# A decoder layer on one core: seven of eleven gate-and-up groups computed as Strassen block products, and the recurrence's stores issued one step later

## The chip, the cores and the metric

The kernel runs on one core of a Trainium2 chip. Five engines work side by side and meet at semaphores: TensorE (PE in the tables; its weight loads are listed apart as PEld), VectorE (DVE), ScalarE (ACT), GpSimd (POOL) and SyncE (SP), which here only issues transfers (DMAs). The metric is the time of one execution on the device in microseconds (us), lower is better.

## The reference, cut to what matters

```python
    lru = _rglru_branch(lru_x, lru_gate, conv_w, conv_b, lru_wa, lru_ba, lru_wi, lru_bi, lru_lambda)
    merged = merge_g[:, :, 0] * (attn @ w_o_attn) + merge_g[:, :, 1] * (lru @ w_o_lru)
    x = x + merged @ w_out
    h2 = _rmsnorm(x, norm2_g)
    return x + (jax.nn.silu(h2 @ w_gate) * (h2 @ w_up)) @ w_down
```

There are 512 tokens and 1024 channels; `w_gate` and `w_up` are 1024 x 2816, `w_down` is 2816 x 1024. All is float32. The recurrence (`_rglru_branch`) is a convolution, two sigmoid gates out of small matrix products, coefficients, a scan over the tokens and a product with a gelu gate.

## The kernel before, in words

**Products.** A float32 operand is cut in two: `hi`, its rounding to the matmul's type (a copy on ACT), and `lo`, the rest (a subtraction on DVE). One product is then three matmuls, hi by hi, lo by hi, hi by lo (`mm3`, lines 197 to 199). Each of them loads its own 128 x 128 weights.

**Weights.** They lie packed in the order of use, in chunks of 128 x 1024 (512 KB). `Weights.load` issues a chunk's transfer on SP into a `raw` tile; `cut_steps` makes `whi` (L165, ACT) and `wlo` (L168, DVE) of it; `get` hands the parts out and cuts and loads some chunks ahead. Five pairs of parts are in flight. Every engine executes its instructions in the order in which the code issues them, so a wait of one instruction holds up all behind it on that engine; SP's transfers too are issued in that order.

**Recurrence.** For each of eight blocks of 128 channels: a projection into a PSUM bank, `lru_conv`, `lru_parts` (hi and lo of the convolved block, L187 and L188), `lru_gates` (six matmuls into two `ps_s` banks), `lru_coeffs` (four ACT functions beginning at L370, then DVE work that ends in `tv` and `av`), `lru_scan`, then `lru_out` and `lru_store` (two transfers of 256 KB into the DRAM tensor `lru_d`). The last blocks overlap with the next stages: four projections `acck` for the compression's keys and values, `blocks_add` and `blocks_split` (tiles `shifted`, `blkh`, `blkl`), then a loop of six steps, each with a projection for the merge gates, `merge_gate` of the step before (ACT L497 reads its bank, SP stores the result in `mg_d`), and one or two chunks of the compression's first layer `w1` (256 columns, into `ps_s`). After it comes the token-major projection of the keys; its four accumulators need all four `ps_dense` banks, the fourth only after `merge_gate(5)` has read it.

**Second norm.** `out_mm` adds the output projection up in eight PSUM banks, two to each of four token blocks. `norm2_sums(t)` adds `x` to them (DVE L1146) and squares and sums (ACT L1147), POOL multiplies by the gain; `norm2_scale(t)` scales; `norm2_t(t)` transposes block t by eight matmuls into two banks and splits them into `h2h` and `h2l`, the norm's result with channels on partitions. `x2`, the sum, stays in SBUF until the end.

**Gate and up.** 22 tiles of 128 output channels, two units each (gate, up); a unit is 8 x 3 matmuls of 512 columns (all tokens). The first three units are split in two halves of 256 tokens, so that they can start while blocks 2 and 3 are still being transposed. After each pair: silu on ACT (L1218), product on DVE (L1219), hi and lo of the result (`gh`, `gl`).

**Down.** Two passes over 22 tiles, each into four token blocks by 512 channels; then `x2` is added and the result stored.

Of the kernel before, what the change touches and what calls it, by code (L numbers as in the profile page):

```python
# [18 lines left out]
P = 128  # L19
# [80 lines left out]
def hybrid_block_kernel(ctx: ExitStack, tc: tile.TileContext, x: bass.AP, wpk: bass.AP,  # L100
# [25 lines left out]
    class Weights:  # L126
# [11 lines left out]
        def load(self, upto):  # L138
            while self.loaded <= min(upto, len(keys) - 1):
# [9 lines left out]
        def cut_steps(self, upto, on_hi=None, on_lo=None, n_steps=1):  # L149
            while self.cut_ <= min(upto, self.stop - 1):  # L150
# [427 lines left out]
    for c in range(N_EARLY):  # L578
        prev, acc = acc, proj_cm(cm("w_in", C_MERGE + P * c), ahead=2)
        if c:  # L580
            merge_gate(c - 1, None, prev)
# [24 lines left out]
        outs = ((), (), (0, 1), (2, 3, 4), (5, 6), (7,))[c]  # L606
# [505 lines left out]
    def late_pool(**kw):  # L1112
        p_, es = open_pool(**kw)
        ctx.enter_context(es)
        return p_

    stage3 = late_pool(name="stage3", bufs=3, side="right")
    x2p = late_pool(name="x2p", bufs=1)
    h2p = late_pool(name="h2p", bufs=1)
    gp = late_pool(name="gp", bufs=28)  # L1120
    fp = late_pool(name="fp", bufs=2, side="right")
    ps = late_pool(name="ps_ffn", bufs=8, space=PSUM)
    PS.clear()
    PS.update(b=8)
    W.stage((stage2, stage3, stage3, stage2, stage3), (stage2, stage3, stage2, stage3), (dve,))
    x2 = x2p.tile([P, NT, D], F32, name="x2")
    for t in range(NT):
        nc.sync.dma_start(x2[:, t, :], x[t * P:(t + 1) * P, :])

    def wkey(name, h, c):  # L1130
        return cols(name, ((512 * h, 512 * h + 512),), 2 * c, 2)

    h2q = [[h2p.tile([P, 4, T], F32R, name=f"h2{m}{b}") for m in "hl"] for b in range(2)]
    h2T = [[m[:, k % 4, :] for m in h2q[k // 4]] for k in range(KT)]
    xn2, sums = {}, {}

    halves = (slice(0, 512), slice(512, D))
    gain2 = [gp.tile([P, 512], F32, tag="g", name="gain2") for _ in halves]
    for sl, g in zip(halves, gain2):
        nc.sync.dma_start(g, rows[:, 640 + sl.start:640 + sl.stop])  # L1140

    def norm2_sums(t):
        xn2[t] = [gp.tile([P, 512], F32, tag="g", name="xn2") for _ in halves]
        ss, v0, w0 = [fp.tile([P, 2], F32, tag="n" + m, name="n" + m, bufs=2) for m in "svw"]
        for h, sl in enumerate(halves):
            dve.tensor_tensor(out=x2[:, t, sl], in0=x2[:, t, sl], in1=acc[t][h], op=OP.add)  # L1146
            act.activation(fp.tile([P, T], F32, tag="sg", name="sq"), x2[:, t, sl], AF.Square,  # L1147
                           accum_out=ss[:, h:h + 1])
            pool.tensor_tensor(out=xn2[t][h], in0=x2[:, t, sl], in1=gain2[h], op=OP.mult)
# [24 lines left out]

    late = 3
# [5 lines left out]
    W.cut(W.used + 1)  # L1181
    for t in range(NT):
# [8 lines left out]
        norm2_sums(t)  # L1191
        if t == 2:
            norm2_t(0)
    norm2_scale(3)


    gT = []
    units = [(n, i) for i in range(FT) for n in ("w_gate", "w_up")]
    early = 3
    w, acc = [], []  # L1200
    for n, i in units[:early]:
        w.append(W.get(cm(n, P * i), KT, ahead=0))
        acc.append(bank("b"))
        mm_cm(acc[-1], w[-1], h2T, lo_half, between=(lambda: norm2_t(len(w))) if len(w) > 1 else None)
    gate_acc = None
    for n, (name, i) in enumerate(units):
        if n < early:
            a = acc[n]
            mm_cm(a, w[n], h2T, hi_half)
            W.cut(W.used)  # L1210
        else:
# [97 lines left out]
```

## Time and profile before

| what | value |
|---|---|
| median of 3 runs | 994.64 us (994.56 to 995.04) |
| the profiled execution | 996.74 us, of which the span of instructions 995.0 us |
| PE busy, and PEld | 976.8 us (98% of the span), 817.1 us |
| DVE busy | 558.2 us (56%) |
| ACT busy | 473.0 us (48%) |
| mean granted TensorE clock | 0.998 of full speed |

The profiled execution is 2.1 us longer than the median and its span 0.4 us longer. A busy share is the time in which an engine had an instruction in work; PE's is modelled from pipelined instructions, so the distance from one start to the next (the pitch) says more than a duration. The stages, by the starts of their first matmuls: recurrence and projections up to about 240 us, attention up to about 575, output projection and second norm up to 620, gate and up 620.1 to 868.5, down 868.5 to 992.

### The profile page before, as it was taken

How to read it: one execution, taken by the hardware profiler on the slowest of the kernel's cores; microseconds unless marked ns; L12 is line 12 of the kernel's file. 1: busy time of each engine (PE TensorE's matmuls, PEld its weight loads, DVE VectorE, ACT ScalarE, POOL GpSimd, SP SyncE). 2: the span in 40 equal slices, each digit the busy share in tenths (PEclk: the TensorE clock that was granted, in tenths of full speed). 3: DMA queues.
4: the chain of work that ended last, by engine and by line, in shares of the span. 5: the costliest groups of instructions: out<-in, count | busy, mean ns of one | idle time of the engine just before them, and what ended most of it. 6: DMA issues, size and time to landing. Idle time of an engine off the chain costs nothing.

```text
span 995.0 us, 13201 instructions
## 1 busy us (share of the span) xinstructions
PE 976.8 (98%) x4915; PEld 817.1 (82%) x4915; DVE 558.2 (56%) x1056; ACT 473.0 (48%) x887; POOL 179.5 (18%) x252
## 2 busy tenths in 40 slices
PE   6999999899999999999999999999999999999998
PEld 6888778788898888888888888988888888888887
DVE  6775998638666787878875545533333333331311
ACT  7556767445655777767763334432223222222110
POOL 2031110113302455545541003100000000000000
PEclk9999999999999999999999999999999999999999
DMA  6321427642223121621214481223222332241501
GB/s 235 99 81 61 135 82 236 228 138 71 73 77 116 44 65 54 223 62 35 64 55 125 139 315 45 85 85 111 101 85 85 93 119 85 85 137 55 172 19 42
DMA packets 34479, 104.84 MB, mean 105 GB/s; under 512 B 3952, under 2 KB 4336, under 8 KB 34416
## 3 DMA queue, kind: packets, MB, share of 16 engines
q1 hardware_dynamic: 34416, 104.01, 32.2%
q8 instruction: 38, 0.62, 0.3%
q14 instruction: 25, 0.20, 0.1%
HBM read 93.51 MB, written 10.49 MB: 105 GB/s over the span
## 4 chain that ended last, share of the span: by engine, by line
PE 79%; DVE 6%; ACT 3%; issue 2%; DMA 1%; ACTq 0%; DVEq 0%
PE ps_b L199 14%; PE ps_b L198 14%; PE ps_b L197 14%; PE ps_dense L1020 10%; PE ps_t L911 4%; PE ps_s L198 2%; PE ps_s L199 2%; PE ps_s L197 2%; PE ps_dense L197 2%; PE ps_dense L199 2%; PE ps_dense L198 2%; PE ps_s L880 2%; PE ps_s L881 2%; PE ps_pv L939 2%; PE ps_pv L938 2%
## 5 line engine op out<-in xcount | busy, mean ns | idle before, releaser
L168 DVE TENSOR_TENSOR wlo<-raw,whi 128x1024 fp32r<-128x1024 f32 (+2 forms) x198 | 185.5, 953 | 109.6 <-ACT whi L165 108.8
L165 ACT CAST whi<-raw 128x1024 fp32r<-128x1024 f32 (+2 forms) x207 | 165.7, 818 | 103.9 <-PE ps_b L199 70.0
L197 PE MATMUL ps_b<-h2h,whi 128*128 128x512 f32 (+1 forms) x376 | 143.4, 381 | 0.0
L199 PE MATMUL ps_b<-h2h,wlo 128*128 128x512 f32 (+1 forms) x376 | 143.2, 381 | 0.0
L198 PE MATMUL ps_b<-h2l,whi 128*128 128x512 f32 (+1 forms) x376 | 143.2, 381 | 0.0
L902 POOL TENSOR_SCALAR p<-p,st,gates 128x128 f32<-128x128 f32 (+3 forms) x128 | 78.5, 626 | 81.0 <-DVE st L898 44.3
L1219 DVE TENSOR_TENSOR sg<-sg,ps_b 128x512 f32<-128x512 f32 x22 | 15.1, 686 | 138.3 <-PE ps_b L199 138.3
L199 PE MATMUL ps_dense<-hth,wlo 128*128 128x512 f32 (+1 forms) x232 | 86.6, 373 | 0.5 <-DVE wlo L168 0.5
L197 PE MATMUL ps_dense<-hth,whi 128*128 128x512 f32 (+1 forms) x232 | 87.0, 375 | 0.0
L198 PE MATMUL ps_dense<-htl,whi 128*128 128x512 f32 (+1 forms) x232 | 86.4, 372 | 0.0
L892 ACT ACTIVATE p<-p,st 128x128 f32<-128x128 f32 (+3 forms) x128 | 72.0, 563 | 24.0 <-DVE st L887 23.4
L199 PEld LDWEIGHTS ps_b<-h2h,wlo 128*128 128x128 f32 x376 | 70.7, 188 | 15.0
L198 PEld LDWEIGHTS ps_b<-h2l,whi 128*128 128x128 f32 x376 | 70.7, 188 | 14.9
L197 PEld LDWEIGHTS ps_b<-h2h,whi 128*128 128x128 f32 x376 | 70.7, 188 | 14.8
L198 PE MATMUL ps_b<-wlo,gh 128*128 128x512 f32 (+1 forms) x198 | 73.2, 370 | 0.0
L199 PE MATMUL ps_b<-whi,gl 128*128 128x512 f32 (+1 forms) x198 | 73.1, 369 | 0.0
L197 PE MATMUL ps_b<-whi,gh 128*128 128x512 f32 (+1 forms) x198 | 73.1, 369 | 0.0
L187 ACT CAST gh<-sg 128x512 fp32r<-128x512 f32 x22 | 13.6, 620 | 123.1 <-DVE sg L1219 123.1
L923 DVE TENSOR_TENSOR ptl<-ps_t,pth 128x512 fp32r<-128x512 f32 x80 | 55.1, 689 | 22.7 <-ACT pth L917 21.7
L887 DVE CUSTOM_DVE_ANT_0 p<-ps_s,bias 128x128 f32<-128x128 f32 (+3 forms) x128 | 61.3, 483 | 10.4 <-PE ps_s L881 7.1
L917 ACT CAST pth<-ps_t 128x512 fp32r<-128x512 f32 x80 | 46.6, 582 | 32.3 <-PE ps_t L911 31.6
L199 PEld LDWEIGHTS ps_dense<-hth,wlo 128*128 128x128 f32 x232 | 43.8, 189 | 9.3 <-DVE wlo L168 0.9
(266 smaller groups left out, 2042.2 us busy)
## 6 DMA issues: line engine op xcount, KB each, us to landing
raw<-in_wpk_dram SPq DMA_DIRECT2D x150, 512.0 KB, 3.6
lru_d<-lt SPq DMA_DIRECT2D x16, 256.0 KB, 4.5
mt<-mg_d SPq DMA_DIRECT2D x16, 256.0 KB, 3.8
mg_d<-mt SPq DMA_DIRECT2D x10, 256.0 KB, 2.1
xt<-in_x_dram SPq DMA_DIRECT2D x4, 512.0 KB, 5.7
lh<-lru_d SPq DMA_DIRECT2D x8, 256.0 KB, 4.1
ll<-lru_d SPq DMA_DIRECT2D x8, 256.0 KB, 4.3
x<-in_x_dram SPq DMA_DIRECT2D x4, 512.0 KB, 6.2
```

Of the source, the lines that this page charges most:

```text
L165: (on_hi or act.copy)(hi[:, sl], raw[:, sl])
L168: eng.tensor_tensor(out=lo[:, sl], in0=raw[:, sl], in1=f(hi[:, sl]), op=OP.subtract)
L197: pe.matmul(acc, lhsT=ah, rhs=bh, start=start, stop=False)
L198: pe.matmul(acc, lhsT=ah, rhs=bl, start=False, stop=False)
L199: pe.matmul(acc, lhsT=al, rhs=bh, start=False, stop=stop)
L887: dve.tensor_tensor_reduce(out=p, in0=accs.pop((h, br, t)), in1=bias[h][:, 384 - t * P:512], scale=-1.0, scalar=3e38, op0=OP.add, op1=OP.m ...
L892: act.activation(p, p, AF.Exp, bias=stat[h][:, 0, br, t:t + 1], scale=-1.0, accum_out=stat[h][:, 1, br, t:t + 1])
L902: pool.tensor_scalar(p, p, sm[:, t:t + 1], gates[:, t, c:c + 1], op0=OP.mult, op1=OP.mult)
L911: pe.transpose(pt[:, o_:o_ + P], probs[h, br, t][:, k * P:(k + 1) * P], ident)
L917: act.copy(ph, pts[h, gi][0])
L923: dve.tensor_tensor(out=pl, in0=pt, in1=f(ph), op=OP.subtract)
L1020: pe.matmul(acc, lhsT=a[l], rhs=b[r], start=start and i == 0, stop=stop and i == 2)
```

## The change

**Gate and up.** Two output tiles (128 channels each, gate and up side by side) make a group; eleven groups. Group 0 is computed plainly, in halves of 256 tokens, as four units (`unit`). Groups 3, 6 and 9 are computed plainly with 512 columns. The other seven are a 2 x 2 block product, weights A (rows: the two tiles, columns: the two halves of the 1024 inputs) by h2 B (rows: halves of the inputs, columns: halves of the tokens), by seven products in place of eight. A product is 24 matmuls for gate and up together (two halves of a bank) by 256 columns. The sums of weights (S1 to S4, 128 x 1024) are made by DVE for each group (`adds`) ahead of their hi and lo; the sums of B (T1 to T4) once, at the end of the second norm (`norm2_t`, `late_sums`, `sum_parts`); the products are added to the four corners by seven additions of 128 x 512 out of PSUM (`post`), and silu and product follow on corners of 256 columns (`gated`). The weights' `raw` tiles now come as pairs (two chunks, three pairs in flight). A step s of the loop issues product s, the sum for s+4, the hi and lo for s+3, and the corner work of s-1. The hi and lo of the results are made later, in the first pass of down (`down_parts`).

**Room.** To make room, `x2` is stored to DRAM (`x2_d`, two buffers in SBUF) and read back near the end of each pass of down; two raw buffers serve the other chunks from the second norm on, where four did; the squares' dump goes into the PSUM bank that was just read.

**Recurrence.** The outputs of two blocks are made at a time (`lru_outs`, lo in place) and their stores issued in the next step (`lru_stores`); the last two come after `merge_gate(5)` and the gelu. `lru_gates(7)` stands one projection later.

```diff
-        for j in outs:
-            lru_out(j)
-        for j in outs:
-            lru_store(j)
+        if 2 <= c < 5:
+            lru_outs(2 * c - 4, 2 * c - 3)
...
+            lru_outs(6, 7)
+            lru_stores()
...
     acck.append(proj_cm(cm("w_in", 1024 + P), ahead=2))
-    lru_gates(7)
     kv_evac(0, acck[0], act.copy)
     lru_scan(4)
     acck.append(proj_cm(cm("w_in", 1024 + 2 * P), ahead=2))
+    lru_gates(7)
...
         prev, acc = acc, proj_cm(cm("w_in", C_MERGE + P * c), ahead=2)
+        lru_stores()
...
-            act.activation(fp.tile([P, T], F32, tag="sg", name="sq"), x2[:, t, sl], AF.Square,
-                           accum_out=ss[:, h:h + 1])
+            act.activation(acc[t][h], v, AF.Square, accum_out=ss[:, h:h + 1])
...
+            bs[t] = [half("b") for _ in range(2)]
+            for d, a in zip(bs[t], pt):
+                act.copy(d, a)
...
+        dve.tensor_tensor(out=t1, in0=pt[0], in1=bs[t - 2][0], op=OP.subtract)
+        dve.tensor_tensor(out=t2, in0=t1, in1=pt[1], op=OP.subtract)
...
+    A_OF = {1: "A11", 2: "A12", 3: "S4", 4: "A22", 5: "S1", 6: "S2", 7: "S3"}
+    B_OF = {1: "B11", 2: "B21", 3: "B22", 4: "T4", 5: "T1", 6: "T2", 7: "T3"}
+    SUMS = {"S1": ("A21", OP.add, "A22"), "S2": ("A11", OP.subtract, "S1"),
+            "S3": ("A21", OP.subtract, "A11"), "S4": ("A12", OP.add, "S2")}
+    NO = FT // 2
+    PLAIN = (0, 3, 6, 9)
+    seq = [(o, p) for o in range(1, NO) for p in ((-1, -2, -3, -4) if o in PLAIN else (1, 5, 2, 6, 7, 3, 4))]
...
+        bh, bl = h2[B_OF[p]]
+        for n in range(2):
+            for k in range(4):
+                sl = slice(512 * n + k * P, 512 * n + k * P + P)
+                mm3(b[:, 256 * n:256 * n + 256], (hi[:, sl], lo[:, sl]), (bh[:, k, :], bl[:, k, :]), k == 0, k == 3)
...
+        elif p == 2:
+            corner(0, 0, 2, 1)
+        elif p == 6:
+            held[2], held[4] = half("u2"), half("u4")
+            add(two(held[2]), 6, 1)
+            add(two(held[4]), 5, 2)
+        elif p == 7:
+            held[3] = half("u3")
+            add(two(held[3]), 7, 2)
+            corner(1, 1, 5, 3)
...
+    def step(s):
+        banks[seq[s][1]] = product(s)
+        adds(s + AHEAD + 1)
+        prep(s + AHEAD)
+        do_later()
+        if s:
+            post(s - 1)
...
+        if t in (1, 2):
+            x2_store(t - 1)
+            x2_load(t + 1)
...
+    AHEAD = 3
+    w, uacc = [], []
+    for n in range(4):
+        i, m = divmod(n, 2)
+        w.append(W.get(cm(("w_gate", "w_up")[m], P * i), KT, ahead=int(n > 0)))
+        uacc.append(bank("b"))
+        unit(uacc[n], w[n], lo_half, {1: lambda: norm2_t(2), 2: lambda: norm2_t(3)}.get(n))
```

Three places show how instructions stand now. The first is on PE in the recurrence's end: the gates of block 7 are the six rows with `ps_s<-lt`, the rows around them are projections into `ps_dense` (`hth`, `htl` are the first norm's parts). Before, they stand between the second and the third of the `acck` projections:

```order
L199 MATMUL ps_dense<-hth,wlo 128x512
L197 MATMUL ps_s<-lt,whi 128x512 [waits Activation_49]
L198 MATMUL ps_s<-lt,whi 128x512 [waits DVE_49]
L199 MATMUL ps_s<-lt,wlo 128x512
L197 MATMUL ps_s<-lt,whi 128x512
L198 MATMUL ps_s<-lt,whi 128x512
L199 MATMUL ps_s<-lt,wlo 128x512
L197 MATMUL ps_dense<-hth,whi 128x512
```

and of the change the same six rows, 24 matmuls (one projection) further on:

```order
L200 MATMUL ps_dense<-hth,wlo 128x512
L198 MATMUL ps_s<-lt,whi 128x512 [waits Activation_49]
L199 MATMUL ps_s<-lt,whi 128x512 [waits DVE_49]
L200 MATMUL ps_s<-lt,wlo 128x512
L198 MATMUL ps_s<-lt,whi 128x512
L199 MATMUL ps_s<-lt,whi 128x512
L200 MATMUL ps_s<-lt,wlo 128x512
L198 MATMUL ps_dense<-hth,whi 128x512 [waits Activation_49]
```

So one projection has moved ahead of them, while on ACT and DVE the coefficients of block 7, which read these banks, keep their place between their neighbours.

The second is on DVE inside gate and up. Before, two units are two `wlo` and one product with its lo:

```order
L168 TENSOR_TENSOR wlo<-raw,whi 128x1024 x2
L1219 TENSOR_TENSOR sg<-sg,ps_b 128x512
L188 TENSOR_TENSOR gl<-sg,gh 128x512
```

Of the change, three steps of a Strassen group that another one follows (`S` is a sum of weights, `c` and `u` corner sums out of PSUM, `g` the silu product; the rows with `wlo` are the lo of a weight or of a sum):

```order
L1254 TENSOR_TENSOR S<-raw_7345,S 128x1024
L189 TENSOR_TENSOR wlo<-raw_7345,whi 128x1024
L1301 TENSOR_TENSOR g<-sg,c 128x256
L1317 TENSOR_TENSOR c<-ps_b,u_7618 128x512
L1254 TENSOR_TENSOR S<-raw_7509,raw_7345 128x1024
L189 TENSOR_TENSOR wlo<-S,whi 128x1024
L1301 TENSOR_TENSOR g<-sg,c 128x256
L1317 TENSOR_TENSOR c<-ps_b,u_7650 128x512
L1254 TENSOR_TENSOR S<-raw_7345,S 128x1024
L189 TENSOR_TENSOR wlo<-S,whi 128x1024
```

Where a unit of 24 matmuls had about two DVE instructions, a product of 24 shorter ones now has about three, 22 to a group.

The third is SP at the second norm. Before, SP has only weights to issue from here on; of the change, the stores and loads of `x` stand between the last two chunks of group 0, and the store of a block ahead of the load that takes its buffer:

```order
L1166 DMA x_d<-x_6148 128x1024 [waits DMAHW2_49,DVE_49]
L1151 DMA x_6404<-in_x_dram 128x1024 [waits DMAHW2_49,DMAHW3_49,Activation_49,Pool_49]
L1166 DMA x_d<-x_6150 128x1024 [waits DMAHW4_49,DVE_49]
L1151 DMA x_6448<-in_x_dram 128x1024 [waits DMAHW4_49,DMAHW5_49,Activation_49,Pool_49]
L145 DMA raw<-in_wpk_dram 128x1024 [waits DMAHW6_49]
L1166 DMA x_d<-x_6404 128x1024 [waits DMAHW7_49,DMAHW3_49,DVE_49]
L1166 DMA x_d<-x_6448 128x1024 [waits DMAHW5_49,DMAHW0_49,DVE_49]
L145 DMA raw<-in_wpk_dram 128x1024 [waits DMAHW1_49]
```

Thus the load of group 0's last chunk stands behind the store that waits for the sum of the last token block.

## Rows read from the trace of the kernel before

**Rows 1.** The page, part 1: busy time of each engine, share, instructions.
```profile
PE 976.8 (98%) x4915; PEld 817.1 (82%) x4915; DVE 558.2 (56%) x1056; ACT 473.0 (48%) x887; POOL 179.5 (18%) x252
```

**Rows 2.** Waits of PE: waiting tile, releaser, us in total, times, longest.
```profile
PE ps_dense L197 <- ACT lt L497: 2.5, 1, 2.5
PE ps_s L198 <- DVE lt L188: 2.0, 2, 1.5
PE ps_dense L199 <- DVE wlo L168: 0.5, 1, 0.5
...
PE ps_s L198 <- DVE wlo L168: 0.3, 1, 0.3
```

**Rows 3.** Timeline of PE: start, duration; first 512-column unit, first of down.
```profile
638.91 0.39 PE L197 MATMUL ps_b<-h2h,whi 128*128 128x512 f32 x1
...
868.51 0.39 PE L197 MATMUL ps_b<-whi,gh 128*128 128x512 f32 x1
```

**Rows 4.** The same, a long stretch of 256-column matmuls, two of its starts.
```profile
629.09 0.28 PE L198 MATMUL ps_b<-h2l,whi 128*128 128x256 f32 x1
...
638.79 0.28 PE L199 MATMUL ps_b<-h2h,wlo 128*128 128x256 f32 x1
```

**Rows 5.** Window: length, busy PE, PEld, DVE, ACT, POOL, clock, DMA; weight loads.
```profile
639.00:868.40 229.40, 229.40 (x985) 184.72 (x984) 76.89 (x82) 63.50 (x82) 0.00 (x0) 1.00 0.30 97
...
L198 PEld LDWEIGHTS ps_b<-h2l,whi 128*128 128x128 f32 x376 | 70.7, 188 | 14.9
```

**Rows 6.** Groups by line and form on DVE: busy us, mean ns.
```profile
L168 DVE TENSOR_TENSOR wlo<-raw,whi 128x1024 fp32r<-128x1024 f32 x42 | 49.6, 1224 | 5.5 <-ACT whi L165 5.5
...
L1219 DVE TENSOR_TENSOR sg<-sg,ps_b 128x512 f32<-128x512 f32 x20 | 13.7, 686 | 127.4 <-PE ps_b L199 127.4
...
L521 DVE TENSOR_TENSOR hu<-hu,hx 128x256 f32<-128x256 f32 x2 | 0.9, 426 | 0.1
```

**Rows 7.** Timeline of DVE: two instructions back to back, 1024 and 512 wide.
```profile
610.28 1.28 DVE L1146 TENSOR_TENSOR x<-x,ps_b 128x512 f32<-128x512 f32 x2
...
638.68 2.36 DVE L168 TENSOR_TENSOR wlo<-raw,whi 128x1024 fp32r<-128x1024 f32 x2 [0.26 <-ACT whi L165]
```

**Rows 8.** Timeline of PE at the recurrence's end, and one window with its clock.
```profile
126.10 0.40 PE L197 MATMUL ps_s<-lt,whi 128*128 128x512 f32 x1
...
147.96 0.39 PE L199 MATMUL ps_dense<-hth,wlo 128*128 128x512 f32 x1
...
193.54 0.50 PE L197 MATMUL ps_dense<-whi,hth 128*128 128x512 f32 x1 [2.48 <-ACT lt L497]
...
180.00:200.00 20.00, 17.52 (x81) 14.28 (x80) 11.71 (x20) 8.34 (x12) 3.04 (x3) 0.91 0.51 184
```

**Rows 9.** Timeline of ACT and DVE there: block 7's first gate, two `wlo`.
```profile
129.28 0.69 ACT L370 ACTIVATE lt<-ps_s,vec 128x512 f32<-128x512 f32 x1
...
140.69 1.22 DVE L168 TENSOR_TENSOR wlo<-raw,whi 128x1024 fp32r<-128x1024 f32 x1
...
145.71 1.22 DVE L168 TENSOR_TENSOR wlo<-raw,whi 128x1024 fp32r<-128x1024 f32 x1
```

**Rows 10.** Timelines at the second norm: DVE, ACT and PE.
```profile
605.27 1.39 DVE L1146 TENSOR_TENSOR x<-x,ps_b 128x512 f32<-128x512 f32 x2 [1.20 <-PE ps_b L199]
...
614.03 1.28 DVE L1146 TENSOR_TENSOR x<-x,ps_b 128x512 f32<-128x512 f32 x2
...
619.44 1.06 ACT L165 CAST whi<-raw 128x1024 fp32r<-128x1024 f32 x1
...
624.38 1.04 PE L1165 MATMUL ps_b<-ident,xn 128*128 128x128 f32 x8
...
624.53 0.62 ACT L1147 ACTIVATE sq<-x 128x512 f32<-128x512 f32 x1
```

**Rows 11.** The page, part 6: transfers, KB each, median us to landing.
```profile
raw<-in_wpk_dram SPq DMA_DIRECT2D x150, 512.0 KB, 3.6
...
x<-in_x_dram SPq DMA_DIRECT2D x4, 512.0 KB, 6.2
```

More of the change, by code (lines that the diff above doesn't have):

```diff
@@ L1109, in hybrid_block_kernel @@
     ps_es.close()
[L1112 to L1122, printed above, removed]
+    stage3, _ = open_pool(name="stage3", bufs=3, side="right")
+    ctx.enter_context(_)
@@ L1126, in hybrid_block_kernel @@
[L1126 to L1135, printed above, removed]
+    ring = (stage2, stage3, stage3, stage2, stage3)
+    first_key = keys.index(cm("w_gate", 0))
@@ new lines, in hybrid_block_kernel, with g_tile, gated, do_later @@
+    graw = {}
+    def g_tile(i):
+        if i not in graw:
+            pool_, tag = (hpool, "h") if i < 16 else (ga, "g")
+            graw[i] = dm if i == FT - 1 else pool_.tile([P, T], F32, tag=tag, name="g")
+        return graw[i]
+    todo = []
+    def gated(i, gate, up, sl=slice(0, T)):
+        sg = half("sg")[:, sl]
+        act.activation(sg, gate, AF.Silu)
+        g = g_tile(i)[:, sl]
+        todo.append(lambda: dve.tensor_tensor(out=g, in0=sg, in1=up, op=OP.mult))
+    def do_later():
+        while todo:
+            todo.pop(0)()
@@ L1170, in out_mm @@
+    def step(s):
[5 more added lines that the diff above has]
+            post(s - 1)
+    for t in range(NT):
+        acc[t] = [bank("b") for _ in range(2)]
     def out_mm(t, k, w):
@@ L1194, in hybrid_block_kernel @@
     norm2_scale(3)
[L1197 to L1209, printed above, removed]
-            W.cut(W.used)
-        else:
-            a = bank("b")
-            mm_cm(a, W.get(cm(name, P * i), KT, ahead=2), h2T)
-        if name == "w_gate":
-            gate_acc = a
-            continue
-        sg = fp.tile([P, T], F32, tag="sg", name="sg")
-        act.activation(sg, gate_acc, AF.Silu)
-        dve.tensor_tensor(out=sg, in0=sg, in1=a, op=OP.mult)
-        pool_, tag = (gp, "g") if i < 14 else (hpool, "h")
-        hi = pool_.tile([P, T], F32R, tag=tag, name="gh")
-        lo = pool_.tile([P, T], F32R, tag=tag, name="gl")
-        split(hi, lo, sg)
-        gT.append((hi, lo))
+    for t in (2, 3):
+        x2_store(t)
@@ new lines, in unit @@
+    def unit(a, w, sl, between=None):
+        for k in range(KT):
+            if between and k == KT // 2:
+                between()
+            mm3(a[:, sl], (w[0][:, k, :], w[1][:, k, :]), [m[:, sl] for m in h2T[k]], k == 0, k == KT - 1)
+    AHEAD = 3
[5 more added lines that the diff above has]
+        unit(uacc[n], w[n], lo_half, {1: lambda: norm2_t(2), 2: lambda: norm2_t(3)}.get(n))
@@ new lines, in hybrid_block_kernel @@
+    prep(0)
+    for t in (2, 3):
+        late_sums(t)
+    sum_parts(1)
+    adds(1)
+    for n in range(4):
+        unit(uacc[n], w[n], hi_half)
+        if n == 0:
+            prep(1)
+            sum_parts(2)
+        elif n == 1:
+            prep(2)
+            sum_parts(3)
+            gated(0, uacc[0], uacc[1])
+        elif n == 2:
+            do_later()
+            sum_parts(4)
+    gated(1, uacc[2], uacc[3])
+    for s in (2, 3):
+        adds(s)
+    W.used = W.cut_ = W.loaded = first_key + 2 * FT
@@ new lines, in hybrid_block_kernel, with down_parts @@
+    W.last = len(keys) - 1
+    gT = {}
+    def down_parts(i):
+        if i < 2:
+            hi, lo = [fp.tile([P, T], F32R, tag="t", name="g" + m) for m in "hl"]
+        else:
+            pool_, tag = (gb, "gb") if i < 16 else (hpool, "h")
+            hi, lo = [pool_.tile([P, T], F32R, tag=tag, name="g" + m) for m in "hl"]
+        split(hi, lo, graw.pop(i))
+        gT[i] = (hi, lo)
+    for s in range(len(seq)):
+        step(s)
+        left = len(seq) - 1 - s
+        if left == 4:
+            W.load(W.used + 1)
+        elif left == 2:
+            W.cut(W.used)
+            do_later()
+            down_parts(0)
+        elif left == 1:
+            W.cut(W.used + 1)
+            do_later()
+            down_parts(1)
```

186 lines of the change are left out of this document (159 added, 27 removed).

## The prediction

> **What bounds the kernel now.** I read the page's busy shares first. PE is at work 98% of the span [rows 1], so a gain must come from fewer or cheaper matmuls or from the few places where PE waits. The list of PE's waits shows only two above half a microsecond that the change touches: 2.5 us for an ACT result and 1.5 us (of 2.0 in two pieces) for a DVE result, both in the recurrence's end; two small ones for `wlo`, 0.8 us together, lie between them [rows 2]. In gate and up PE waits for nothing: 984 matmuls of 512 columns lie between the two starts of [rows 3], (868.51 - 638.91) / 984 = 0.2333 us each. In that window DVE works 76.9 of 229.4 us [rows 5], so DVE has room. The price of a 256-column matmul stands where the first units are split: 82 lie between the two starts of [rows 4], 9.70 / 82 = 0.1183 us. Half the columns cost 50.7% of the time, although each matmul loads its own weights and one such load is listed with 188 ns [rows 5].
>
> **Gate and up: columns.** A plain group is 96 matmuls of 512 columns, 96 x 0.2333 = 22.40 us. A Strassen group is 7 x 24 = 168 of 256 columns, 168 x 0.1183 = 19.87 us. That is 2.53 us less, seven times 17.7 us. The fourth unit of group 0 is now split too: 48 x 0.1183 - 24 x 0.2333 = +0.1. Sum: -17.6 us, if PE never waits.
>
> **Gate and up: DVE.** This work must hide behind the 19.87 us. A group's 22 DVE instructions are 7 `wlo` and 4 sums (1024 wide), 7 corner additions out of PSUM (512), 4 products (256). By durations [rows 6] that is 11 x 1.224 + 7 x 0.686 + 4 x 0.426 = 20.0 us. Back to back, two 1024-wide ones took 2.36 us and two 512-wide ones 1.28 [rows 7], a pitch of 1.18 and 0.64; by these it is 11 x 1.18 + 7 x 0.64 + 4 x 0.43 = 19.2 us. So DVE needs 97 to 101% of a Strassen group's time: it becomes the second bound, with no reserve of its own. What covers it is the lead and the plain groups. Weights are prepared three products ahead, 3 x 24 x 0.1183 = 8.5 us, and a plain group asks only 4 x 1.22 + 2 x 0.69 = 6.3 us of DVE in 22.4. Strassen groups come at most two in a row, so DVE loses at most 2 x (20.0 - 19.87), 0.3 us, within the lead. I take 0 for it.
>
> The Trainium skill, page "VectorE: DVE Perf Modes", section "The DRAIN you can't avoid", says that the next instruction does not start until the pipe has emptied. By it the durations, 20.0 us, would count; the pair in [rows 7] took less than two durations, so the row does not agree for instructions that need nothing from each other. Either sum leaves the forecast as it is.
>
> Two chunks per tile must also come for each group, 4 x 512 KB in 19.9 us, while one lands in 3.6 us [rows 11]. In a pair of Strassen groups the second tile of the next group can only be fetched once S4 has freed its buffer, at the beginning of the group, and is wanted three products (8.5 us) later; two chunks of 3.6 us, one after the other, are 7.2 us. Free, with little to spare; by the slowest such row, 6.2 us each, 3.9 us too late for DVE.
>
> ACT's part is 7 copies, one evacuation and 4 silus, less than half the group; it is no bound. The hi and lo of the results move to the first pass of down, where DVE has 1.2 + 2 x 0.7 = 2.6 us to do in 24 matmuls of 0.2333, 5.6 us. Free. There two raw buffers give each chunk 11 us; a load of 3.6 us and a cut of 2.3 fit. The last addition and store are as before.
>
> **The second norm.** Three things are added ahead of the moment when PE asks for block 2's transposes (624.38 [rows 10]). ACT copies two transposed banks for each of blocks 0 and 1; a 512-wide one is half of a 1024-wide copy of 1.06 us [rows 10], so 1.1 us for block 1 lies just ahead of the chunk's copy at 619.44 and shifts the chain behind it: scale, sum and square of block 3. Its banks are those that the transposes need, and now the square writes into them, so they are free at the end of the second square, 624.53 + 0.62 + 1.1 = 626.3, where the second four transposes would come at 624.8. PE waits 1.5 us. Second, the load of group 0's last chunk stands on SP behind the store that waits for block 3's sum: that is whole when the second square begins, 624.53 + 1.1 = 625.6. Issued then and landed after 4 to 6 us, with two stores ahead of it [rows 11], copied (1.06) and subtracted (1.22), it is ready by 632 to 634. PE wants it after the transposes (two sets of 0.8, with the 1.5 us of waiting), three half units and two matmuls: 624.4 + 1.5 + 1.6 + 38 x 0.1183 = 632.0. I take 0.8, nearer to the early end. Third, `x` of block 2 comes after the store of block 0 (the sum is there at 605.27 + 1.39 = 606.7): two transfers of 3.6 us, 613.9, wanted at 614.03 [rows 10, 11]. By the rows at either side, twice 3.6 or twice 6.2, it is on time or 5.1 us late; I take 0, since both have the size of the chunk's. The T sums (4 subtractions, 4 additions, 8 lo, 10.4 us by 0.65) and three weights' parts must be made by DVE in the 8 x 24 x 0.1183 = 22.7 us of group 0's units; they fit, but with some 1.2 us to spare in the first pair. Sum: +2.3 us, bounds 0 and 7.
>
> **The recurrence.** The 1.5 us wait for `lt` [rows 2], just behind the gates' first matmul at 126.10 [rows 8], goes, since PE runs a projection meanwhile. But the gates now begin at 126.1 + 24 x 0.2333 = 131.7, their first bank is whole at about 132.6, and ACT's gate function, at 129.28 [rows 9], starts 3.3 us later. On DVE the coefficients, `shifted` and then the two `wlo` of [rows 9] stand behind it in order, with hardly a gap: they shift by 3.3 us. PE, 1.5 us early, wanted the second of them at 147.96 [rows 8]; it was done at 146.9 and is now done at 150.2. So PE is 2.2 us late there in the sum, and pauses some 3 us. The idle of 2.48 us ahead of 193.54 [rows 8] was followed by the clock's fall: the window 180 to 200 has a granted clock of 0.91, 0.09 x 20 = 1.8 us lost at 1.2 GHz, while the 1.5 us behind 126.10 were followed by no fall. I take 1.8 us here. Later the two small `wlo` waits go, -0.8, since PE comes later than they do. Then the wait of 2.5 us at 193.54 goes with its 1.8 us of clock, -4.3: `merge_gate(5)` now stands ahead of the last output on ACT, and the stores no longer hold the weights' loads. Sum: +2.2 + 1.8 - 0.8 - 4.3 = -1.1 us. Bounds: -6.6, if the chain loses nothing, and +3.2, if the old wait stays with the new.
>
> **The sum.** Against the profiled span: 995.0 - 17.6 + 2.3 - 1.1 = 978.6 us. The median is 0.4 us below that span, so 978.2 us.
>
> **The rivals.**
> 1. DVE or its weights hold PE up in the Strassen groups. For it: 97 to 101% by rows, many of the 22 wait for another DVE result, and the second group of a pair can wait for its raw tile. Against it: the lead and the plain groups. If each instruction cost 0.1 us more, a group would need 22.2, 2.3 us too much; of a pair's 4.6 the lead takes 4 (1.2 in the first): 3.4 + 0.6 + 0.6 = 4.6 us in three pairs. With the raw tile 2 us late in each pair, 6 more. 983, up to 989.
> 2. The recurrence's chain loses nothing and the second norm does not wait: -6.6 + 0 in place of -1.1 + 2.3. For it: the 2.5 us are surely cut short. Against it: the shift of 3.3 us has no gap to vanish in. About 970 to 975.
> 3. The other side: the 256-column pitch does not hold. In long runs of short matmuls the weight load could set the pace; its place is every product. It decides at 22.40 / 168 = 0.1333 us, 13% above the row, where all of the 17.6 us is gone; at the load's own 0.188 us a group takes 31.6 us, +9.2 x 7 = +64, and 17.6 less gain nothing: about 1060. Against it: 82 in a row at 0.1183.
>
> The Trainium skill, page "TensorE: Matmul & The Clock Gate", section "The mechanism", says that a weight load overlaps with running matmuls only when the row group differs; here all fill the array, so by it rival 3 would hold. The trace does not agree: loads of 188 ns go on inside a pitch of 0.1183.
>
> **How the numbers follow.** The forecast 0.56 (its own range 975.5 to 981.5), rival 1 0.22, rival 2 0.18, rival 3 0.02, another loss that eats the gain 0.02. No more than 2 in 10 left out: 971 to 986.5. A change of 0.2%, 2 us, is about what a measurement can tell here. Faster 0.96, same 0.01, slower 0.03.
>
> **What would show it.** Right: the span of a Strassen group in PE starts 19.9 us; DVE busy over 90% there; no PE wait on `wlo` or `S` after group 0; one PE wait of some 3 us for the `wlo` near 147 us with a lower clock behind it, none at 190; one on the squares near 625. Wrong: PE waits in each second group of a pair (rival 1); a pitch above 0.12 us (rival 3); a wait at the second norm for the load of `x`, which would be late by more than I allow.

## The result, and the profile after

The changed kernel takes 983.37 us (median of 4 runs, 982.0 to 985.76) against 994.84 us (4 runs, 994.56 to 998.12): a ratio of 0.988, 95% interval 0.9866 to 0.9895, so 11.5 us less. The forecast was 978.2, 5.2 less than was measured; the time lies within 971 to 986.5, but above the forecast's own band of 975.5 to 981.5. The profiled execution has a span of 984.0 us, 5.4 more than the sum's 978.6. It is the slowest of the four, 2.4 us above their median.

The page of the changed kernel, part 1 (as [rows 1]):

```profile
PE 962.8 (98%) x5443; PEld 833.3 (85%) x5443; DVE 654.4 (67%) x1184; ACT 506.1 (51%) x941; POOL 177.8 (18%) x252
```

DVE has 96 us more to do and PE 14 less, yet PE is as busy as before. Next, the longest waits of PE (as [rows 2]; two of 7.7 and 0.9 us in the first 10 us of the kernel are left out, they are there before the change too):

```profile
PE ps_dense L200 <- DVE wlo L169: 3.1, 2, 2.8
PE ps_dense L198 <- ACT whi L166: 1.1, 1, 1.1
...
PE ps_b L198 <- ACT whi L166: 0.8, 1, 0.8
PE ps_dense L199 <- DVE wlo L169: 0.8, 1, 0.8
PE ps_b L200 <- DVE wlo L169: 0.8, 1, 0.8
```

All of these are for a weight's parts, and none is for an `S`: its lo is made in line 189, and no wait for a `wlo` of that line is in the whole list. To see where each lies, read the starts on PE's timeline:

```profile
149.67 0.50 PE L200 MATMUL ps_dense<-hth,wlo 128*128 128x512 f32 x1 [2.79 <-DVE wlo L169]
...
151.40 0.63 PE L200 MATMUL ps_dense<-hth,wlo 128*128 128x512 f32 x1
...
202.46 0.49 PE L198 MATMUL ps_dense<-whi,hth 128*128 128x512 f32 x1 [1.13 <-ACT whi L166]
203.72 0.50 PE L199 MATMUL ps_dense<-wlo,hth 128*128 128x512 f32 x1 [0.77 <-DVE wlo L169]
...
621.78 0.39 PE L199 MATMUL ps_b<-h2l,whi 128*128 128x256 f32 x1 [0.15 <-DVE h2l L189]
...
626.02 0.60 PE L1191 MATMUL ps_b<-ident,xn 128*128 128x128 f32 x4
627.02 0.63 PE L1191 MATMUL ps_b<-ident,xn 128*128 128x128 f32 x4 [0.40 <-DVE xn L1173]
...
630.80 1.09 PE L1191 MATMUL ps_b<-ident,xn 128*128 128x128 f32 x8 [0.32 <-ACT xn L1172]
...
634.14 0.38 PE L198 MATMUL ps_b<-h2h,whi 128*128 128x256 f32 x1 [0.82 <-ACT whi L166]
635.40 0.44 PE L200 MATMUL ps_b<-h2h,wlo 128*128 128x256 f32 x1 [0.76 <-DVE wlo L169]
635.64 0.41 PE L198 MATMUL ps_b<-h2h,whi 128*128 128x256 f32 x1
...
650.99 0.28 PE L198 MATMUL ps_b<-h2h,whi 128*128 128x256 f32 x1
...
690.75 0.39 PE L198 MATMUL ps_b<-h2h,whi 128*128 128x512 f32 x1
...
857.34 0.39 PE L198 MATMUL ps_b<-whi,gh 128*128 128x512 f32 x1
```

The wait at 149.67 is the one that was forecast near 147; the two at 202 to 204 and the two at 634 to 636 were not, or not in this size. Durations of 0.63 and 0.41 us, where the same shapes take 0.39 and 0.28 elsewhere, mark a fallen clock, behind 149.67 and behind 635.40. The windows, with the granted clock as the third number from the end, say the same; 0.50 is the lower level, 1.2 GHz:

```profile
140.00:160.00 20.00, 17.21 (x79) 13.97 (x79) 15.27 (x13) 17.28 (x23) 0.00 (x0) 0.91 0.47 125
...
636.00:638.50 2.50, 2.50 (x14) 2.50 (x13) 2.46 (x4) 1.14 (x2) 0.00 (x0) 0.50 0.00 0
```

From 650.99 (group 1's first product) to 690.75 two Strassen groups take 39.76 us, 19.88 each. The windows of these two groups, as [rows 5], show no idle time of PE, with DVE (third engine) at 18.85 and 16.24 us:

```profile
650.99:670.87 19.88, 19.88 (x171) 19.88 (x170) 18.85 (x22) 8.72 (x11) 0.00 (x0) 1.00 0.29 106
670.87:690.75 19.88, 19.88 (x171) 19.88 (x170) 16.24 (x22) 8.77 (x12) 0.00 (x0) 1.00 0.44 158
```

From such starts the span divides into stages (before: the fourth unit of gate and up ends at 638.91 + 24 x 0.2333 = 644.51):

| stage, by starts on PE | before | after | difference |
|---|---|---|---|
| up to the gates near 100 us | 100.15 | 100.60 | +0.45 |
| gates near 100 to the keys' fifth bank (215.14; 216.34) | 114.99 | 115.74 | +0.75 |
| to the first matmul of gate and up (620.12; 621.35) | 404.98 | 405.01 | +0.03 |
| first four units, with the second norm's transposes | 24.39 | 29.64 | +5.25 |
| the other ten groups | 224.00 | 206.35 | -17.65 |
| down and the end | 126.49 | 126.66 | +0.17 |

The columns gave what they were to give. The second norm (5.15 us, without the 0.1 of columns in that row) and the recurrence (+0.75, in the second row) took back more than was summed.

### The profile page after: what moved, and what is told of

Same layout as the page of the kernel before. It is cut to its first block, busy times and chain, and to the rows that moved or that the text cites. A ratio compares the mean times of both kernels' runs of the same rounds, so it can differ in the third digit from the quotient of the medians.

```text
span 984.0 us, 14464 instructions
## 1 busy us (share of the span) xinstructions
PE 962.8 (98%) x5443; PEld 833.3 (85%) x5443; DVE 654.4 (67%) x1184; ACT 506.1 (51%) x941; POOL 177.8 (18%) x252
## 4 chain that ended last, share of the span: by engine, by line
PE 76%; DVE 6%; ACT 3%; DMA 3%; issue 2%; SPq 0%; ACTq 0%; DVEq 0%
PE ps_b L200 13%; PE ps_b L199 13%; PE ps_b L198 13%; PE ps_dense L1028 10%; PE ps_t L919 4%; PE ps_dense L199 2%; PE ps_dense L200 2%; PE ps_dense L198 2%; PE ps_s L199 2%; PE ps_s L200 2%; PE ps_s L198 2%; PE ps_s L888 2%; DMA raw<-in_wpk_dram 2%; PE ps_s L889 2%; PE ps_pv L947 2%; PE ps_pv L946 2%
## 5 line engine op out<-in xcount | busy, mean ns | idle before, releaser
L169 DVE TENSOR_TENSOR wlo<-raw,whi 128x1024 fp32r<-128x1024 f32 (+2 forms) x158 | 138.6, 885 | 96.0 <-ACT whi L166 95.6
L166 ACT CAST whi<-raw 128x1024 fp32r<-128x1024 f32 (+2 forms) x167 | 126.1, 764 | 100.2 <-PE ps_b L200 52.6
L198 PE MATMUL ps_b<-h2h,whi 128*128 128x256 f32 (+1 forms) x328 | 104.2, 318 | 0.8 <-ACT whi L166 0.8
L200 PE MATMUL ps_b<-h2h,wlo 128*128 128x256 f32 (+1 forms) x328 | 104.0, 317 | 0.8 <-DVE wlo L169 0.8
L199 PE MATMUL ps_b<-h2l,whi 128*128 128x256 f32 (+1 forms) x328 | 103.9, 317 | 0.2 <-DVE h2l L189 0.2
L931 DVE TENSOR_TENSOR ptl<-ps_t,pth 128x512 fp32r<-128x512 f32 x80 | 55.1, 689 | 22.8 <-ACT pth L925 21.8
L198 PEld LDWEIGHTS ps_b<-h2h,whi 128*128 128x128 f32 x328 | 62.5, 191 | 5.5 <-ACT whi L166 1.0
L200 PEld LDWEIGHTS ps_b<-h2h,wlo 128*128 128x128 f32 x328 | 62.5, 190 | 5.3 <-DVE wlo L169 1.0
L199 PE MATMUL ps_b<-h2lt,whi 128*128 128x256 f32 x224 | 62.9, 281 | 0.0
L200 PE MATMUL ps_b<-h2ht,wlo 128*128 128x256 f32 x224 | 62.9, 281 | 0.0
L198 PE MATMUL ps_b<-h2ht,whi 128*128 128x256 f32 x224 | 62.9, 281 | 0.0
```

The costliest lines, as they stand in the source:

```text
L166: (on_hi or act.copy)(hi[:, sl], raw[:, sl])
L169: eng.tensor_tensor(out=lo[:, sl], in0=raw[:, sl], in1=f(hi[:, sl]), op=OP.subtract)
L198: pe.matmul(acc, lhsT=ah, rhs=bh, start=start, stop=False)
L199: pe.matmul(acc, lhsT=ah, rhs=bl, start=False, stop=False)
L200: pe.matmul(acc, lhsT=al, rhs=bh, start=False, stop=stop)
L931: dve.tensor_tensor(out=pl, in0=pt, in1=f(ph), op=OP.subtract)
```

## The experiments

Each time below is a median, with the lowest and highest run. The kernel before took 994.6 to 995.7 us beside them. All edits are to the changed kernel.

**1. The chunk ahead of the last outputs.** The keys' projection waits at 202.46 for a `whi`. ACT's timeline of the changed kernel shows what stands ahead of it:

```profile
198.73 0.42 ACT L530 ACTIVATE hu<-hu 128x256 f32<-128x256 f32 x1 [2.13 <-DVE hu L529]
200.24 1.22 ACT L395 CAST lt<-lt 128x512 fp32r<-128x512 f32 x2 [1.10 <-DVE lt L394]
201.37 1.99 ACT L166 CAST whi<-raw 128x1024 fp32r<-128x1024 f32 x2
```

Behind the gelu (L530) come the two outputs that the change moved there (L395), after a wait of 1.10 us for DVE, and only then the chunk.

```diff
+            W.cut(W.used + 2)
             lru_outs(6, 7)
             lru_stores()
```

> The next weight chunk of the keys' projection is cut ahead of the last two outputs of the recurrence, on ACT and DVE; all else as in the changed kernel. Theory A (the two outputs, moved behind the gelu, hold up the chunk's whi by 3.1 us on ACT): the waits of 1.13 and 0.77 us near 201 to 204 us go, the time falls by about 2.3 us, 983.4 to 981.1. Rival B (the chunk's parts are late for its transfer, or the next chunk is, so the wait only moves): a wait of like size shows at this or the next chunk, the time stays within 0.5 us.

981.62 us (981.4 to 982.38). Both waits are gone; ACT cuts the chunk right behind the gelu, and the outputs follow:

```profile
197.97 1.03 ACT L166 CAST whi<-raw 128x1024 fp32r<-128x1024 f32 x1
200.90 1.23 ACT L395 CAST lt<-lt 128x512 fp32r<-128x512 f32 x2 [1.90 <-DVE lt L394]
```

The stage from the first matmul of the keys' projection to its fifth bank falls from 26.88 to 24.17 us by the starts on PE; before the change it took 28.43. So A holds, with 1.8 us on the medians and 2.7 in the stage.

**2. The gates of block 7 back in their place,** with the edit of 1.

```diff
     acck.append(proj_cm(cm("w_in", 1024 + P), ahead=2))
+    lru_gates(7)
     kv_evac(0, acck[0], act.copy)
     lru_scan(4)
     acck.append(proj_cm(cm("w_in", 1024 + 2 * P), ahead=2))
-    lru_gates(7)
```

> As the run that cuts the chunk ahead of the last outputs, and the gates of block 7 at their old place, one projection earlier. Theory A (moving the gates cost more than the 1.5 us wait that it removed: the wait of 2.8 us near 149 and the lower clock behind it are its doing, and the bank that merge_gate(5) must read is no longer late): the time falls by 1.5 to 3 us against the run without it (981.6), to 979 to 980. Rival B (what PE gains there it loses again at merge_gate(5) near 190 us, since the chunks' transfers set that stage's pace): a wait of 2 to 3 us for merge_gate(5) is back, and the time is within 0.7 us of 981.6.

978.97 us (977.55 to 981.78), 2.65 less than without it. The 1.5 us wait near 128 is back, the one of 2.8 with its lower clock is gone, and the wait for `merge_gate(5)` (its tile is `lt`, line 505) does not return. On PE and ACT of this run:

```profile
190.70 0.39 PE L200 MATMUL ps_dense<-whi,htl 128*128 128x512 f32 x1
191.22 0.50 PE L198 MATMUL ps_dense<-whi,hth 128*128 128x512 f32 x1
...
189.62 1.05 ACT L166 CAST whi<-raw 128x1024 fp32r<-128x1024 f32 x1 [4.29 <-DMA raw<-in_wpk_dram]
190.58 0.59 ACT L505 ACTIVATE lt<-ps_dense 128x512 f32<-128x512 f32 x1
```

PE asks for the bank at 190.9 and goes on at 191.22, 0.3 us later; in [rows 8] it went on at 193.54, after 2.48 us. On ACT of the kernel before, the last output's copy (L389), which waits for DVE, stands ahead of `merge_gate(5)` (L497):

```profile
192.37 0.62 ACT L389 CAST lt<-lt 128x512 fp32r<-128x512 f32 x1 [1.95 <-DVE lt L388]
192.90 0.59 ACT L497 ACTIVATE lt<-ps_dense 128x512 f32<-128x512 f32 x1
```

So it was the new place of the last outputs, behind `merge_gate(5)`, that removed that wait; moving the gates only lost.

**3. The recurrence as before,** all else changed (the first four pieces of the diff above and the place of the gates, reversed).

> The recurrence as in the kernel before (outputs, stores and the place of the gates of block 7), gate and up as in the changed kernel. Theory A (read from the profile after: the recurrence's part cost some 0.8 us in all, because the chunk behind the last outputs came late): the time falls by about 0.8 us, to 982.6. Rival B (the term of the prediction, a gain of 1.1 us): the time rises by 1.1 us, to 984.5. In either case the waits of 1.5 us near 128 and 2.5 us near 193 are back and the one of 2.8 us near 149 is gone.

981.14 us (980.58 to 982.54): 2.2 us less than the changed kernel, whose fastest run lies within these, so the recurrence's edits gain nothing as they stand and seem to cost some 2 us. More than A expected, probably for this reason: the wait near 193 is back with 2.40 us, but without the clock's fall that [rows 8] shows behind it (granted clock 0.91 there, 1.00 here in the same window).

```profile
193.65 0.50 PE L198 MATMUL ps_dense<-whi,hth 128*128 128x512 f32 x1 [2.40 <-ACT lt L500]
...
180.00:200.00 20.00, 17.60 (x87) 14.43 (x87) 11.76 (x20) 8.23 (x12) 3.04 (x3) 1.00 0.55 189
```

The profile of before was thus one with a fall that need not come, and the table's +0.75 us sets a fall of after against one of before. The granted clocks of all 38 executions of the kernel before, run beside these experiments, bear this out: 11 have 0.998, as the profiled one, and took 996.1 to 998.1 us; 27 have 1.0 and took 993.9 to 996.2.

**4. The last two chunks of group 0 loaded first.** In the changed kernel SP's timeline and what follows from it on ACT and DVE read so:

```profile
617.54 0.42 SPq L145 DMA_DIRECT2D raw<-in_wpk_dram  x1
618.07 10.36 SPq L1166 DMA_DIRECT2D x_d<-x  x2
628.48 0.42 SPq L145 DMA_DIRECT2D raw<-in_wpk_dram  x1
...
619.33 1.18 ACT L1197 COPY b<-ps_b 128x512 f32<-128x512 f32 x2 [0.27 <-DVE h2l L189]
...
621.76 1.19 ACT L1197 COPY b<-ps_b 128x512 f32<-128x512 f32 x2 [0.27 <-DVE h2l L189]
623.08 1.05 ACT L166 CAST whi<-raw 128x1024 fp32r<-128x1024 f32 x1
...
626.80 1.27 DVE L1158 TENSOR_TENSOR x<-x,ps_b 128x512 f32<-128x512 f32 x2
...
633.04 1.04 ACT L166 CAST whi<-raw 128x1024 fp32r<-128x1024 f32 x1 [1.34 <-DMA raw<-in_wpk_dram]
```

Two pairs of copies and a `whi` stand ahead of the scale of block 2, so block 3's sum comes at 626.80, its store and the last chunk behind it at 628.48, and the `whi` at 633.04.

```diff
     W.cut(W.used + 1)
+    W.load(W.used + 3)
     for j in (2, 3, 4):
         raw_load(j)
```

> The last two chunks of group 0 are loaded ahead of the stores and loads of x, in buffers that are free by then. Theory A (they come late because they stand on SP behind stores and loads that wait for the sums): the waits of 0.82 and 0.76 us near 634 and 635 us go, and with them the lower clock behind them (16 matmuls at 0.21 in place of 0.118 us); group 0 takes 25 to 26 us in place of 29.6, the time falls by 3.4 to 4.5 us, to about 979.5. Rival B (the transfers' number is the limit, not their order): x comes later instead, PE waits for the transposes, and the time falls by less than 1 us.

992.23 us (991.22 to 994.25): 9 us slower. The loads must wait for buffers, and with them on SP everything behind:

```profile
592.35 13.48 SPq L145 DMA_DIRECT2D raw<-in_wpk_dram  x5
605.89 3.17 SPq L1239 DMA_DIRECT2D raw<-in_wpk_dram  x6
609.16 0.78 SPq L1166 DMA_DIRECT2D x_d<-x  x1
620.83 0.33 SPq L1151 DMA_DIRECT2D x<-in_x_dram  x1
```

The six raw tiles start 7 us later (605.89; in the changed kernel 598.75), the first store of `x` is issued behind their 3 MB, and the load of block 2, which takes that store's buffer, comes at 620.83 in place of 611.68: PE waits 8.9 us for the first `h2h`. The waits for `whi` and `wlo` are gone, but that says nothing here.

**5. The same loads between `x` of block 2 and the store of block 1.**

```diff
             x2_load(t + 1)
+        if t == 1:
+            W.load(W.used + 3)
```

> The last two chunks of group 0 are loaded behind the load of x for block 2 and ahead of the store of block 1, in place of behind the store that waits for the last sums. Theory A (order on SP): the waits for whi and wlo near 634 us (0.3 to 0.8 and 0.8 to 1.0 us) go, block 3's chain is up to 1.5 us earlier, x still comes in time; group 0 takes 25.5 to 26.5 us, the time falls by 1.5 to 3.5 us from 983.4, to 980 to 982. Rival B (each transfer moved ahead makes another late): x of block 3 comes late, PE waits for the last transposes, and the time falls by less than 0.7 us or rises.

983.37 us (983.0 to 984.74), no change: B's time without B's cause, since block 3's sum did not wait for its `x`. The wait for `whi` went; the one for `wlo` grew to 1.51 us, and DVE shows why:

```profile
631.81 0.68 DVE L1202 TENSOR_TENSOR t<-ps_b,b 128x512 f32<-128x512 f32 x1
632.52 0.69 DVE L1203 TENSOR_TENSOR t<-t,ps_b 128x512 f32<-128x512 f32 x1
633.13 1.22 DVE L169 TENSOR_TENSOR wlo<-raw,whi 128x1024 fp32r<-128x1024 f32 x1
```

The chunk had landed, but its `wlo` stands behind block 2's split and two sums for T, without a gap. So the order on DVE and ACT holds PE up as much as the load does.

**6. That order changed too.** Copies later, chunks cut earlier (the core of the edit; it also loads the two chunks ahead of the stores of `x`, and DVE, not POOL, makes the third chunk's lo):

```diff
             if t == 3 and k == late - 1:
+                norm2_scale(2)
+                W.cut(W.used + 2)
                 norm2_t(1)
...
     norm2_scale(3)
+    W.cut(W.used + 3)
+    copies(1)
```

> The second norm of the changed kernel in another order, nothing left out: block 2 is scaled and the third chunk cut ahead of block 1's transposes, the fourth chunk is cut ahead of block 2's split, the copies of blocks 0 and 1 stand behind the sums that wait on ACT, and the two chunks are loaded ahead of the stores of x. Theory A (what delays PE there is the order of ACT and DVE: two copies of 1.2 us and a whi ahead of block 2's scale, the split and the sums T of block 2 ahead of the fourth chunk's wlo): the waits for whi and wlo near 634 us go, gate and up with group 0 takes 231 to 232 us in place of 234 to 236, the time falls by 2 to 3.5 us, to about 980.5. Rival B (the stores and loads of x set the pace): PE waits for the transposes of block 2 or 3, or for the first split, as long as it waited for the chunk, and the time is within 0.7 us of 983.4.

983.83 us (983.16 to 987.19), again no gain, although gate and up by itself falls from 235.99 to 232.17 us by the starts, as A expected. No wait for `whi` or `wlo` is left, but now the first units wait for block 1's split, which had been put behind a scale and a cut:

```profile
623.16 0.38 PE L198 MATMUL ps_b<-h2h,whi 128*128 128x256 f32 x1 [0.77 <-ACT h2h L188]
624.54 0.39 PE L199 MATMUL ps_b<-h2l,whi 128*128 128x256 f32 x1 [1.00 <-DVE h2l L189]
```

B's effect without B's cause: what is waited for is not a transfer of `x`, but ACT and DVE in another order.

**7. All ten groups as Strassen groups.** `PLAIN = (0,)`.

> Groups 3, 6 and 9 are Strassen groups too; only group 0 is plain. Theory A (columns set the pace, and DVE, busy 18.5 to 18.9 of 19.9 us in a Strassen group that another one follows, just holds): three groups fall from 22.40 to 19.87 us, 7.6 us in all, to about 975.8, with no new PE wait. Rival B (the plain groups between are what lets DVE and the raw tiles catch up): PE waits for S, wlo or raw tiles in the later groups, 2 us or more a group, and the time falls by less than 4 us or rises.

978.32 us (977.45 to 978.98), 5.05 less on the medians. By the starts on PE, the ten groups behind group 0 fall from 206.35 to 198.80 us, 7.55 where A's 7.6 stood; no product of them waits. Down takes 1.0 us more, with a new wait of 0.6 us for a `gl`; why the medians show only 5.05 is not clear beyond that. Seven groups in a row, in one window:

```profile
693.00:832.00 139.00, 139.00 (x1177) 139.00 (x1176) 129.03 (x153) 61.86 (x84) 0.00 (x0) 1.00 0.30 107
```

DVE is busy 129.03 / 7 = 18.4 of 19.86 us a group, 93%. The plain groups are not needed.

**8 and 9. DVE's work raised,** S1 to S3 made twice, in the changed kernel and with ten Strassen groups.

```diff
-            dve.tensor_tensor(out=a_of(o, name), in0=a_of(o, a), in1=a_of(o, b), op=op)
+            for _ in range(2 if name != "S4" else 1):
+                dve.tensor_tensor(out=a_of(o, name), in0=a_of(o, a), in1=a_of(o, b), op=op)
```

> The changed kernel, in which DVE makes S1, S2 and S3 of each Strassen group twice (three more instructions of 128 x 1024, 3.5 us more, some 22.0 us of DVE in 19.9). Theory A (the lead of three products and the plain groups carry two such groups in a row): a pair loses 2 x 2.1 us, less than the lead of 8.5 us, and only the first pair, which starts with less lead, may show: 0 to 3 us above 983.4. Rival B (DVE has no slack beyond its own time): 2.1 us in each of seven groups, 15 us.

988.38 us (988.28 to 989.78), 5.0 more: PE waits 3.1 us for the lo of sums, all in groups 1 and 2, the later pairs behind a plain group not at all.

> The same with all ten groups as Strassen groups. Theory A: without plain groups the lead is used up once: ten groups lose 21 us, less 8.5 of lead, 10 to 14 us above the run with ten groups (978.3), about 990, with PE waiting for wlo of S in every product of the later groups. Rival B (DVE's busy share hides more overlap than the pitch shows, and DVE still keeps up): 978 to 981.

1005.55 us (1004.67 to 1007.61), 27 more than run 7; 23 waits for the lo of sums, 19.6 us. Seven groups here:

```profile
705.78:865.43 159.65, 144.65 (x1179) 140.43 (x1177) 154.35 (x176) 62.22 (x85) 0.00 (x0) 1.00 0.26 93
```

A group takes 22.8 us, DVE works 22.05 of it, 97%: it sets the pace. Both runs lost more than expected. The lead of 8.5 us that I had counted is not there in group 1, where PE waits for the first time 9.7 us after its start in run 8; and in run 9 a group loses 2.9 us, not the 2.2 by which DVE's work exceeds the products, for a reason that stays open.

**10. All groups plain.** `PLAIN = tuple(range(NO))`.

> All groups of gate and up plain, all else (the recurrence, the store and reload of x2, the sums T, which nothing uses then) as in the changed kernel. Theory A (a Strassen group saves what its columns save, 22.40 less 19.87 us, and nothing more or less): 7 x 2.53 = 17.7 us above the changed kernel, about 1001; so all the rest of the change costs some 6 us against 994.8. Rival B (Strassen groups carry hidden costs that plain ones don't, or the rest costs less): below 998.

1003.1 us (1001.17 to 1004.78), 19.7 more than the changed kernel, so A's 17.7 within some 2 us, the spread of these runs. By the starts the ten groups take 224.00 us, as in the kernel before, and 206.35 in the changed one: 17.65. What the change does beside the products costs 7.4 us against the kernel before (995.71 beside this run).

**11 and 12. Together.** Run 11 is 1's, 2's, 6's and 7's edits; run 12 the same with block 1's split ahead of block 2's scale again.

> All together: ten Strassen groups, the gates at their old place, the chunk cut ahead of the last outputs, and the second norm in the new order. Theory A (the parts add): 978.97 (gates and cut) less 5 to 7.6 (three more Strassen groups) less 2 to 3.5 (norm), 968 to 972. Rival B (with fewer waits ahead the next bound shows: DVE in ten Strassen groups in a row, or transfers of raw tiles): 974 or more, with new waits for wlo in gate and up.

973.22 us (971.15 to 976.4), ratio 0.9779 (0.9759 to 0.9798).

> As the run with all fixes, but block 1's transposes and split stand again ahead of block 2's scale and the third chunk's cut. Theory A (each piece of ACT and DVE work put ahead of the split makes the first half unit late by its own length): the two waits at the first half unit (1.5 and 1.0 us in the run with all fixes) go and no wait for whi or wlo comes back, 2 to 2.9 us less, 970 to 971.5. Rival B (the work of the second norm on ACT and DVE is as long as PE's time there, whatever its order): the wait comes back at block 3's transposes or the fourth chunk, and the time is within 0.7 us of 973.2.

972.83 us (972.11 to 973.58), ratio 0.9778 (0.9764 to 0.9791). Both take some 10 us less than the changed kernel and 22 less than the kernel before. Run 11 lies above A's 968 to 972: the time of run 2 less the gain of run 7 is already 973.9, which leaves the second norm's edits 0.7 us, less than the runs differ. In run 12 the waits at the first split are gone (one of 0.76 us, for a copy, is left), but the time is the same, as B expected: by the starts the ten groups take 1.0 us more, and the first pass of down now waits 1.7 us for `gl` and `gh`, 0.6 in run 11. What the second norm still costs could not be brought out of the total.

## Why the prediction was right, and where not

**Columns, DVE.** Right to 0.1 us: -17.55 measured for -17.6, no wait in any Strassen group. Rival 3 fell: the pitch was 0.1183 in every product. DVE's need was sized too high, 18.4 to 18.9 us a group where 19.2 to 20.0 stood; in the second group of a pair, which a plain one follows, it was 16.2, so the sign "over 90%" held in the first only. The cover named for it, a lead of 8.5 us, is not there in the first pair (runs 8, 9), and the plain groups, also named, are not needed (run 7). In the window of run 7 DVE's durations sum to 138.9 us in 129.0 of busy time, so instructions overlap. The Trainium skill, page "VectorE: DVE Perf Modes", section "The DRAIN you can't avoid", has the next one start when the pipe is empty, but adds that one which is not held starts earlier; these rows agree with the section only with this addition, which the prediction left out.

**Recurrence, -1.1 us: wrong in sign.** The late `wlo` came as worked out (2.79 us, and a granted clock of 0.91 in the window 140 to 160, 1.8 us; a pause of some 3 us and the same clock were forecast); from the gates near 100 up to the first matmul of the keys' projection PE lost 2.3 us (86.56 before, 88.86 after) where 3.2 were summed. The step that failed is "the wait of 2.5 us at 193.54 goes with its 1.8 us of clock, -4.3". It went, and run 1 shows the 4.3 in full by the profiles (28.43 to 24.17); of the two reasons that were given, run 2 shows the order on ACT, and nothing shows that the stores had held the loads. But the last outputs that were moved behind `merge_gate(5)` stood ahead of the next chunk's cut on ACT and DVE, and PE lost 2.7 us of it again at 202 to 204. I had asked who waits for `merge_gate(5)`, not who waits behind the outputs in their new place. The same step also took the 1.8 us of clock for a part of every execution. The size is 0.75 us by the two profiles and 2.2 by run 3; the difference, some 1.5 us, is about one fall of the clock, which the profile of before has and 27 of the 38 executions do not.

**Second norm, +2.3 us: mis-sized, 5.15.** By the starts on PE, each distance less its pitch, the 5.15 us are: 0.4 behind the first matmul, for block 1's split; 0.55 each for an `xn` at the transposes of blocks 2 and 3; 2.0 at the chunk, whose waits are 0.82 + 0.76, not 0.8; and 1.6 for the clock that fell behind it, most of it the 16 matmuls from 635.40 to 638.84, 3.44 less 16 x 0.1183, 1.5 us. That fall is this execution's: in the other seven profiles with this order of group 0 it is absent, and group 0 takes 27.7 to 28.8 us, 3.3 to 4.4 over the 24.39 of before.

Two steps failed. "Its banks are those that the transposes need", 1.5 us, did not come: the transposes of block 2 began at 626.02, ahead of block 3's sum at 626.80, which still had its banks to read; so they wrote other banks, and what PE waited for was block 2's scale. And "1.1 us for block 1 lies just ahead of the chunk's copy" counted only half: both pairs of copies, 1.2 us each, pushed block 2's scale back, so block 3's sum came at 626.80, 3.6 us after this one of before's trace, of which 1.2 is the shift of the whole stage:

```profile
623.19 1.27 DVE L1146 TENSOR_TENSOR x<-x,ps_b 128x512 f32<-128x512 f32 x2
```

The last chunk's load stood behind that sum, as was said, and its `wlo` had its own queue on DVE (run 5), which the sum did not name. That these two orders are all that holds PE up there is argued, not shown: runs 4 to 6 removed or moved the waits for the chunk, and none gained.

**The sum.** 978.6 + 1.85 (recurrence) + 2.85 (norm) + 0.1 (columns) + 0.6 (start and end) = 984.0. The time fell into rival 1's band, but rival 1 did not happen: no wait for DVE's parts or for a raw tile lies in a Strassen group. That it stayed within 971 to 986.5 owes more to the smallness of these two terms beside 17.6 than to their working, and is luck as far as they go.

## What to carry to other kernels

Where an instruction is moved, ask twice who queues behind it: at the old place, whose wait goes, and at the new one, whose wait begins; here 2.7 of the 4.3 us that went came back on the same engine. In a stage where ACT, DVE and the queue of transfers each keep their order, moving one piece forward (runs 4 to 6) did not pay, because what it passed came late in its turn: load, cut and sums are one chain. The block product gave in full the 2.5 us a group that 1 in 8 columns less are worth here, where the engine that adds had work for 93% of the products' time (run 7); where it had 22.05 us of work for 19.87 us of products, it set the pace (run 9). Nothing was tried between the two. What came with it here, room for its tiles, the sums of h2 and the recurrence's new order, cost 7.4 us (run 10).

## What the runs showed of the hardware

The clock's fall to 1.2 GHz does not follow from the length of a wait alone. Behind the 2.8 us at 149 it came in all nine profiles that have this wait, behind the 2.4 to 2.5 us at 193 in one of two, behind the pair of waits at 202 to 204 (0.8 to 1.1 and 0.8 us) in three of eight, behind the pair at the chunk near 634 (0.3 to 0.8 and 0.8 to 1.0 us) in one of eight, and behind the 1.5 us at 128 in none of five. Even the first is not certain: of the 40 executions of those nine kernels, 35 had a mean granted clock of 0.998 or less, one had 0.999 and four had 1.0, too high for a whole fall. One such fall costs 1.5 to 1.8 us (0.91 granted over 20 us), where the runs of one kernel differ by 1 to 5 us here. Also, in long runs of 256-column matmuls weight loads of 190 ns were listed at a pitch of 0.1183 us without slowing it, for all 168 matmuls of a group and, in run 7, for 1680 in a row.
